# A two-trunk encoder layer on one core: stores of neighbourhood attention by SyncE, strips dealt per unit, a weight load behind rope rows, two token sums in another tile

## The chip, the cores and the metric

One Trainium2 chip, and one of its cores. The metric is the device time of one execution in microseconds, the median of the runs shown. Lower is better. A core has five engines that work beside each other, each in the order of its own queue: TensorE (PE in the profile), VectorE (DVE), ScalarE (ACT), GpSimd (POOL) and SyncE (SP, which issues transfers and computes nothing). ACT and POOL can issue transfers too.

## The reference

One encoder layer, run on two inputs with shared weights: `x_prompt` (1024 tokens, the "long" trunk) and `x_sample` (512 tokens, the "short" trunk), both 1024 wide, float32. Cut to what matters:

```python
def _token_mixer(xn, ...):
    z = xn @ w_in                     # q_A k_A v_A q_B k_B v_B gate_A gate_B
    qa = rope(rmsnorm(qa)); ka = rope(rmsnorm(ka))
    o_a = _gqa_attention(qa, ka, va)              # all tokens, 8 heads
    o_b = _neighbourhood_attention(qb, kb, vb, rpb)   # 8 heads, a window of the token grid
    merged = sigmoid(ga) * (o_a @ w_proj_a) + sigmoid(gb) * (o_b @ w_proj_b)
    return merged @ w_out

def _trunk(x, ...):
    h = x + _token_mixer(_rmsnorm(x, norm_mix_g), ...)
    h = h + (relu(_rmsnorm(h, norm_mlp_g) @ w_mlp_up) ** 2) @ w_mlp_down
    return _rmsnorm(h, norm_final_g)
```

The neighbourhood attention takes 128 queries at a time against a band of rows of the 64-wide token grid, adds a learned bias per head and 2-D offset, masks what is outside the window, and takes the softmax.

## The kernel before

**Arithmetic.** Every float32 product is made of three PE products of a high and a low part (`mm3`, whose one line is L216, so nearly all of PE's rows carry that line). High parts come from ACT (L203 for weights, L1594 in the MLP), low parts from DVE (L210, L1595).

**Stages.** `run` works the short trunk (number 0 in the program's names, NT=4 token tiles, NB=1), then the long one (number 1, NT=8, NB=2). Each has four: R (norm, rotary rows, projections, in two groups g), A (global attention), B (neighbourhood attention, 32 units of head h and query block j in the order 1, 2, 0, 3), G (gated merge, `w_out`, the sum with x, the norm for the MLP). One MLP over all tokens follows.

**What orders the work.** Within the code's dependences a scheduler of the framework sets the order on each engine at build, by its own estimate of costs. `tc.keep_in_program_order` and `tc.issue_after` pin an instruction. On the chip each engine then runs its fixed list. Transfers issued by SP and ACT share eight completion semaphores, dealt in turn at build: an issue also waits until the transfer that had its semaphore before has landed, and whatever stands behind it on its engine waits too.

**Short B.** For a head, `prep` fetches its bias rows (`rects`, L1080) and 16 value strips (`vss`, L1094, from the DRAM scratch `vds`). A unit then is: scores (`sbs`, PE), bias, mask and maximum (DVE L1193), exponential (ACT L1222, out `pbs`), scaling of the rows (POOL L1225), transposition (PE L1266, back into `sbs`), high and low parts (ACT L1273, DVE L1274), and values times weights (`obs<-bhs,vss`, PE). `finish_o` copies the outcome (ACT L482, `ot_Bs`) and stores it to the scratch `obds`. Between units PE takes pieces of gate products (`gpss`, out `sgs`, ACT L470), which are stored to the scratch `zgs`. Both stores go through `put` (L441), here from ACT's queue. POOL builds the next head's masked bias (`bms`, L1173) and copies key rows by a transfer (L1157).

**Long R, g=0.** For token tile tt: the tile `xts` (L280) is squared and normed (ACT L300, DVE L304), transposed (PE L317, `ptxs`), split (ACT L327, DVE L333), multiplied (`zs`); then rotary rows `rts` (L745, three buffers) enter on POOL L705 and DVE L716, and ACT L721 makes `rrs`, which PE transposes (L642, `pqs`). The first gate weights of g=0 (`raw_gs`, 512 KB, L249) are asked for by `fill.pull(1)` in the code of tile 6; the scheduler had put the load ahead of the fifth tile's.

**Long G, second half, token tiles 4 to 7.** The tile `xrs` (x's columns, L1487) gets the `w_out` product added (DVE L1527) and is stored by POOL (L1528, `hd<-xrs`). It lies in the ring `k4` of four tiles. The norm's weights `gb` (`gbms`) are last read at tile 3 of this half. In the MLP's start, `S` and `A` tiles lie on memory that G has left: the fifth and seventh `A` of the first products on that of tiles 6 and 7.

Of the kernel before, what the change touches and what calls it, by code (L numbers as in the profile page):

```python
# [61 lines left out]
def encoder(ctx: ExitStack, tc: tile.TileContext, xs, outs, w):  # L62
# [362 lines left out]
    def run(tr, nxt, first):  # L425
        N, x, T, NT, NB = tr.N, tr.x, tr.T, tr.NT, tr.NB
# [8 lines left out]
        fill = Fill()  # L435
        later_put, slot_no = [], [None]
# [109 lines left out]
        for g in range(2):  # L546
            with phase(f"phR{N}_{g}") as ph:
                xn_of, pre = {}, {}
                fresh = g == 0 and tr.ready < NT
                if fresh and not first:  # L550
# [13 lines left out]
                    gb = ph.tile([P, 1, D], F32, tag="gb", name=f"gb{N}", bufs=1)  # L564
                    row_bcast(gb, w["norm_mix_g"], D)
                    gb = gb[:, 0]
# [3 lines left out]
                elif fresh:  # L570
                    gb = ph.tile([P, D], F32, tag="gb", name=f"gb{N}", bufs=1)
# [149 lines left out]
                        nc.scalar.activation(rr[:, i, :], t[:, h, :], AF.Copy, scale=r[:, h : h + 1])  # L721
                    rr_of[tt] = rr

                lag, x_rest = [], []
                for tt in range(NT):
                    tb, j = divmod(tt, 4)
                    nm = f"{N}_{g}_{tt}"
                    def next_tile():
                        rest = tr.p0_t(tt + 1, xn_of.pop(tt + 1))
                        if not first:  # L730
                            x_rest[:] = [rest]
                        if not first and tt + 3 < NT:
                            next_norm(tt + 3)
                        elif first and tt + 2 < NT:
                            step = held.pop(0) if held else None
                            xn_of[tt + 2] = tr.p0(tt + 2, ph, gb, xt_of.get(tt + 2), step)
                            while held:
                                held.pop(0)()

                    to_come = fresh and tr.ready <= tt + 1 < NT  # L740
                    in_z = first and to_come and tt > 0
                    if to_come and not in_z:
                        next_tile()
                    rt = pre.pop("rt", None) or ph.tile([P, 2, HD], F32, tag="rt", name=f"rt{nm}", bufs=3)
                    op = nc.sync.dma_start(rt, w["rope"][tt * P : (tt + 1) * P])  # L745
                    if first and fresh and tt < 2:
                        tc.keep_in_program_order(op)
                    z = mm(f"z{nm}")[:, :384]
                    js = slice(j * P, (j + 1) * P)

                    for c0, c1 in ((0, 256), (256, 384)) if first and g + tt == 0 else ((0, 384),):
                        for k in range(NC8):
                            mm3(
                                z[:, c0:c1],
                                xh(tb, k)[:, js],
                                xl(tb, k)[:, js],
                                wh[k // 4][:, k % 4, c0:c1],
                                wl[k // 4][:, k % 4, c0:c1],
                                k == 0,
                                k == NC8 - 1,  # L760
                            )
                            if in_z and k == 2:
                                next_tile()
                    if tt >= 2:
                        values(tt - 2)
                        heads_t(tt - 2)
                    lag.append(partial(chain, tt, z, rt))
                    if not (first and fresh) or tt > 0:
                        lag.pop(0)()
                    if tt == NT - 1:  # L770
                        while lag:
                            lag.pop(0)()
                    if fresh and not first:
                        if tt == 0:
                            xn_of[tr.ready] = norm_to(xn_next, xt, gb, f"{N}_{tr.ready}")
                            tr.p0_t(*tr.carry.pop(0))
                        if tt == 1:
                            next_norm(tr.ready + 1)
                    if first and g == 0 and tt == 1:
                        load_pad()  # L780
                    if tt == NT - 2:
                        fill.add(gate(2304, zg[0], g * 4, g * 4 + 4))
                        fill.pull(1)

                if g == 0:
                    warm_table(AF.Exp, rr_of[NT - 1][:, 0, 0:1], f"e{N}")
# [11 lines left out]
            with phase(f"phA{N}_{g}") as ph:  # L798
# [148 lines left out]
                else:  # L947
# [4 lines left out]
                    for ui, u in enumerate(units):  # L952
                        h, qb = u
# [106 lines left out]
        with phase(f"phB{N}") as ph:  # L1060
# [4 lines left out]
            n = len(units)  # L1065
            moved = set(units[: n - 8]) if NB == 2 else set()
# [6 lines left out]
            def prep(h):  # L1073
                prep_bias(h)
                for j in range(4):
                    prep_v(h, j)

            def prep_bias(h):
                rc = ph.tile([P, 16, 48], F32, tag="rect", name=f"rect{N}_{h}", bufs=2)
                nc.sync.dma_start(rc, biases[:, :, h].rearrange("r c i j -> (r c) i j"))  # L1080
                rects[h] = rc
# [249 lines left out]
                due_t.setdefault(i + ls, []).append(u)  # L1331
                due_v.setdefault(i + ls + 1, []).append(u)
            for i in range(n + 4 - NB):
                if moved:
                    slot_no[0] = i
                if i < n - 8:
                    f = (5 if i < 2 else 2 + i % 2) if NB == 1 else 5 - (i % 6 == 5)
                else:
                    f = 3 if NB == 1 else 8
                if NB == 2 and i == n - 11:  # L1340
                    pa = proj_a(ph, raw_here)
                    next(pa)
                spare.clear()
                if i < n:
                    late = i > 0 and units[i - 1] in moved
                    if i > 1 and units[i - 2] in moved:
                        fetch_t(units[i - 2])
                    s_unit(units[i], partial(turn, units[i - 1]) if late else None)
                    h, j = units[i]
                    if j == 1 and h < 7:  # L1350
                        if moved:
                            prep_bias(h + 1)
                        else:
                            prep(h + 1)
                    if moved and h > 0:
                        with behind("SP"):
                            prep_v(h, j)
                    if i % 8 == 6 and i + 2 < n:

                        qp = qkproj(i // 8 + 1, wqk, qk)  # L1360
                        for _ in range(NC8):
                            next(qp)
                    if i % 8 == 7 and qp is not None:
                        for _ in qp:
                            pass
                        qp = None
                        if i + 1 < n - 8:
                            wqk = load_qk(i // 8 + 2, held)
                if NB == 2 and i == n - 7:
                    for u in due_v.pop(i):  # L1370
                        v_unit(u)
                    fill.drain()
                    fill.add(pa)
                fill.pull(f // 2)
                for u in due_t.get(i, ()):
                    t_unit(u)
                if NB == 1 and i == n - (12 if first else 8):
                    pa = proj_a(ph, raw_here)
                    next(pa)
                if NB == 1 and i == n - 8:  # L1380
                    fill.drain()
                    fill.add(pa)
                if held and (i in (4, 5) if i < 8 else i % 8 in (2, 4)):
                    held.pop(0)()
                if i == 3:
                    wqk = load_qk(1, held)
                if oa_held and i >= (n - 9 if NB == 2 else n - 11):
                    oa_held.pop(0)()
                if qp is not None and NB == 2:
                    for _ in range(NC8):  # L1390
                        next(qp)
                fill.pull(f - f // 2)
                for u in due_v.get(i, ()):
                    v_unit(u)
                if NB == 2 and oa_held and i >= n - 9:
                    oa_held.pop(0)()
                while later_put and later_put[0][0] < i:
                    nc.sync.dma_start(*later_put.pop(0)[1:])
# [8 lines left out]
        with phase(f"phG{N}") as ph:  # L1407
# [55 lines left out]
            gb = ph.tile([P, 1, D], F32, tag="gb", name=f"gbm{N}", bufs=1)  # L1463
            row_bcast(gb, w["norm_mlp_g"], D)
            gb = gb[:, 0]
# [7 lines left out]
            for half in range(2):  # L1473
                wo = wos[half]
                hc = slice(half * 512, half * 512 + 512)
                for tt in range(NT):
                    tb, j = divmod(tt, 4)
# [2 lines left out]
                    rows_ = slice(r0, r0 + P)  # L1480

                    later = half == 1 and nxt is None and tb == 1
                    if later:
                        xr = ph.tile([P, D], F32, tag="k4", name=f"xr{nm}", bufs=4)[:, 0:512]
                    else:
                        xr = tmp_zs(f"xr{nm}")
# [44 lines left out]
                    if half == 1:  # L1531
# [12 lines left out]
                        else:  # L1544
# [10 lines left out]
                            if 3 <= tt <= 5:  # L1555
                                j = tt - 3
# [563 lines left out]
```

## Time and profile before

| | |
|---|---|
| median of 3 runs | 2090.06 us (2089.89 to 2092.77) |
| the profiled execution | 2093.47 us |
| its span, first to last instruction | 2091.7 us |
| mean granted PE clock | 0.998 |
| busy: PE, DVE, ACT, POOL | 2067.3, 1457.4, 1140.2, 447.4 us |

All times in the profile are of the one profiled execution, in us from its span's start. A timeline row reads: start, duration, engine, line, operation, `out<-in`, shapes, how many in a row; the bracket at its end is the engine's idle time just before and what ended it. A queue's name ends in q (SPq, ACTq) where the row is the issue of a transfer. Names are the program's, with their numbers left out.

### The profile page before, as it was taken

What the parts mean: (1) busy time and instruction counts of PE and PEld (TensorE: products, weight loads), DVE (VectorE), ACT (ScalarE), POOL (GpSimd) and SP (SyncE); (2) the same over time, 40 slices, a digit from 0 to 9 for tenths busy, and PEclk for the clock granted to TensorE, in tenths of its full rate; (3) what the DMA queues carried; (4) which work ended last, traced back from release to release, by engine and by line L of the source; (5) the groups of instructions that cost most, each with busy time, mean ns of one, the idle gap of its engine ahead of it and who ended that gap; (6) DMA issues with size and microseconds to landing.
All of it is one profiled execution on the core that took longest, in us unless ns stands there. A gap on an engine that the chain in (4) does not pass through costs nothing.

```text
span 2091.7 us, 31228 instructions
## 1 busy us (share of the span) xinstructions
PE 2067.3 (99%) x10615; PEld 1813.4 (87%) x10615; DVE 1457.4 (70%) x2691; ACT 1140.2 (55%) x2455; POOL 447.4 (21%) x556
## 2 busy tenths in 40 slices
PE   9999999999999999999999999999999999999998
PEld 8887778887898788888888999999999988888887
DVE  6665786778448646778845777787777777669663
ACT  6674663668557735556413565565656634334442
POOL 2323310317724753443002000011000000000000
PEclk9999999999999999999999999999999999999999
DMA  6537557548628867767544556487545899678561
GB/s 194 148 112 198 168 161 254 190 136 223 169 66 217 215 182 212 219 224 215 186 167 166 183 176 211 152 246 208 159 151 161 291 334 348 216 263 277 170 211 61
DMA packets 407910, 409.99 MB, mean 196 GB/s; under 512 B 98367, under 2 KB 334919, under 8 KB 407751
## 3 DMA queue, kind: packets, MB, share of 16 engines
q1 hardware_dynamic: 368119, 339.16, 52.6%
q10 hardware_dynamic: 29408, 41.96, 5.9%
q0 software_dynamic: 10224, 26.88, 4.9%
q8 instruction: 84, 1.38, 0.3%
q14 instruction: 75, 0.61, 0.1%
HBM read 294.21 MB, written 114.49 MB: 195 GB/s over the span
## 4 chain that ended last, share of the span: by engine, by line
PE 77%; DVE 1%; issue 1%; DMA 1%; ACT 1%; POOL 0%; SPq 0%; POOLq 0%; DVEq 0%; ACTq 0%
PE dn L216 20%; PE gpss L216 8%; PE ud L216 6%; PE ua L216 6%; PE uc L216 6%; PE ops L216 3%; PE ub L216 3%; PE zs L216 2%; PE ppbs L216 2%; PE pqbs L216 2%; PE pkbs L216 2%; PE ppas L216 2%; PE zvs L216 2%; PE dnf L216 2%; PE ss L810 1%; PE ss L811 1%
## 5 line engine op out<-in xcount | busy, mean ns | idle before, releaser
L216 PE MATMUL dn<-wd,ah 128*128 128x512 f32 x1248 | 384.1, 389 | 0.0
L216 PEld LDWEIGHTS dn<-wd,ah 128*128 128x128 f32 x1248 | 234.3, 188 | 48.4
L216 PE MATMUL dn<-wd,al 128*128 128x512 f32 x624 | 242.8, 389 | 0.0
L1594 ACT ACTIVATE ah<-ar 128x512 fp32r<-128x512 f32 x168 | 103.8, 627 | 193.9 <-PE dn L216 174.4
L216 PE MATMUL gpss<-xs_0h,w_gs 128*128 128x512 f32 x512 | 185.5, 399 | 0.0
L1595 DVE TENSOR_TENSOR al<-ar,ah 128x512 fp32r<-128x512 f32 x168 | 113.9, 686 | 71.7 <-ACT ah L1594 63.8
L216 PE MATMUL ud<-B,A 128*128 128x384 f32 x768 | 145.0, 337 | 2.3 <-DVE c L1712 2.3
L216 PE MATMUL uc<-B,A 128*128 128x384 f32 x768 | 143.7, 334 | 0.0
L216 PE MATMUL ua<-B,A 128*128 128x384 f32 x768 | 139.0, 334 | 0.0
L216 PEld LDWEIGHTS dn<-wd,al 128*128 128x128 f32 x624 | 117.2, 188 | 24.4
L216 PEld LDWEIGHTS ud<-B,A 128*128 128x128 f32 x768 | 135.1, 189 | 2.6 <-DVE c L1712 2.6
L216 PEld LDWEIGHTS uc<-B,A 128*128 128x128 f32 x768 | 134.0, 188 | 0.2 <-ACT A L1594 0.2
L216 PEld LDWEIGHTS ua<-B,A 128*128 128x128 f32 x768 | 134.0, 188 | 0.2
L180 POOL TENSOR_TENSOR rs_f<-ms_f,mhalf 128x1 f32<-128x1 f32 x6 | 4.0, 666 | 590.7 <-DVE ms_f L176 590.7
L813 DVE TENSOR_REDUCE nms<-ss 128x1 f32<-128x1024 f32 (+1 forms) x96 | 99.3, 1037 | 32.5 <-PE ss L811 32.2
L216 PE MATMUL ops<-wh_os,mgs 128*128 128x512 f32 x384 | 119.5, 391 | 0.0
L822 ACT ACTIVATE ps<-ss,nms 128x1024 f32<-128x1024 f32 (+1 forms) x96 | 93.3, 973 | 38.5 <-DVE nms L813 37.4
L216 PEld LDWEIGHTS gpss<-xs_0h,w_gs 128*128 128x128 f32 x512 | 96.0, 188 | 17.4
L216 PE MATMUL gpss<-xs_0l,w_gs 128*128 128x512 f32 x256 | 101.0, 394 | 0.0
L1594 ACT ACTIVATE A<-S 128x512 fp32r<-128x512 f32 x128 | 75.9, 623 | 32.1 <-DVE S L1657 23.3
L216 PE MATMUL gpss<-xs_1h,w_gs 128*128 128x512 f32 x256 | 90.8, 393 | 0.0
L1225 POOL TENSOR_SCALAR pbs<-pbs,rlbs 128x384 f32<-128x384 f32 (+1 forms) x96 | 72.1, 756 | 85.1 <-DVE rlbs L1224 75.4
(309 smaller groups left out, 5161.0 us busy)
## 6 DMA issues: line engine op xcount, KB each, us to landing
ar<-ud SPq DMA_DIRECT2D x120, 512.0 KB, 5.5
br<-in_w_mlp_down_dram SPq DMA_DIRECT2D x72, 512.0 KB, 5.4
rawu<-in_w_mlp_up_dram SPq DMA_DIRECT2D x64, 512.0 KB, 4.1
ud<-c ACTq DMA_DIRECT2D x128, 192.0 KB, 3.4
raw_gs<-in_w_in_dram SPq DMA_DIRECT2D x32, 512.0 KB, 3.9
tas<-ps SPq DMA_DIRECT2D x32, 512.0 KB, 3.3
hqs<-tas SPq DMA_DIRECT2D x32, 512.0 KB, 5.5
ud<-cs SPq DMA_DIRECT2D x64, 192.0 KB
```

Of the source, the lines that this page charges most:

```text
L180: op = nc.gpsimd.tensor_tensor(r[:, :n], m[:, :n], mhalf[:, :n], op=ALU.pow)
L216: op = nc.tensor.matmul(out, a, b, **kw)
L810: nc.tensor.matmul(s[:, ks], lhs, kT[:, 0, ks], start=True, stop=False)
L811: nc.tensor.matmul(s[:, ks], lhs, kT[:, 1, ks], start=False, stop=True)
L813: nc.vector.tensor_reduce(nm_, s, axis=AX.X, op=ALU.max, negate=True)
L822: op = nc.scalar.activation(to, of, AF.Exp, bias=nm_, accum_out=l)
L1225: nc.gpsimd.tensor_scalar(p, p, rl, 1.0, op0=ALU.mult, op1=ALU.mult)
L1594: nc.scalar.activation(hi, src, AF.Copy)
L1595: nc.vector.tensor_tensor(lo, src, hi.bitcast(F32), op=ALU.subtract)
```

## The change

Three places, in four edits.

1. Short B, stores: for the first 16 of the 32 units `put` no longer issues from ACT but leaves the store in `later_put`, which the loop empties into SP's queue one unit later. The last 16 units store from ACT as before.
2. Short B, strips: the next head's bias rows are still asked for at its predecessor's first unit, but its 16 strips are dealt four to a unit (`prep_v(h + 1, j)`).
3. Long R, g=0: the first gate-weight load is held back with `tc.issue_after` until the issue of the fourth tile's rotary rows.
4. Long G, second half: token tiles 6 and 7 put their sums into the two halves of `gb`'s tile in place of two tiles of the ring.

```diff
-                lag, x_rest = [], []
+                lag, x_rest, ropes = [], [], []
...
                     op = nc.sync.dma_start(rt, w["rope"][tt * P : (tt + 1) * P])
+                    ropes.append(op.ins)
...
                         fill.add(gate(2304, zg[0], g * 4, g * 4 + 4))
-                        fill.pull(1)
+                        with tc.issue_after(ropes[3]) if fresh and not first else nullcontext():
+                            fill.pull(1)
...
             for i in range(n + 4 - NB):
-                if moved:
-                    slot_no[0] = i
+                slot_no[0] = i if moved or i < n // 2 else None
...
                     if j == 1 and h < 7:
-                        if moved:
-                            prep_bias(h + 1)
-                        else:
-                            prep(h + 1)
+                        prep_bias(h + 1)
+                    if not moved and h < 7:
+                        prep_v(h + 1, j)
...
                     later = half == 1 and nxt is None and tb == 1
-                    if later:
+                    if later and tt >= NT - 2:
+                        xr = gb[:, (tt - NT + 2) * 512 : (tt - NT + 3) * 512]
+                    elif later:
                         xr = ph.tile([P, D], F32, tag="k4", name=f"xr{nm}", bufs=4)[:, 0:512]
```

`moved` is empty in the short trunk and holds units in the long one, so edits 1 and 2 leave the long B as it was. Lines behind L724 shift by up to two in the changed kernel (L1222 is L1224 there, L441's stores on SP carry L1398).

**ACT in short B, about the first gate store.** In a row before (the numbers behind `pbs` are trunk, head, query block):

```order
L203 ACTIVATE w_gs0_3328_2_2291<-raw_gs0_3328_2_0_2289 128x1024
L470 ACTIVATE sgs0_3328_0_0_2286<-gpss0_3328_0_0_2246 128x512
L441 DMA zgs0_1_100<-sgs0_3328_0_0_2286 128x512
L1222 ACTIVATE pbs0_0_0_2307,lbs0_0_0_0_2308<-sbss0_0_0_0_2304,nmbs0_0_0_0_2305 128x256
L1273 ACTIVATE bhs0_0_1_2316<-sbs0_0_0_2299 128x2x128
```

and now:

```order
L203 ACTIVATE w_gs0_3328_2_2282<-raw_gs0_3328_2_0_2280 128x1024
L470 ACTIVATE sgs0_3328_0_0_2278<-gpss0_3328_0_0_2234 128x512
L1224 ACTIVATE pbs0_0_0_2298,lbs0_0_0_0_2299<-sbss0_0_0_0_2295,nmbs0_0_0_0_2296 128x256
L1275 ACTIVATE bhs0_0_1_2311<-sbs0_0_0_2290 128x2x128
L1224 ACTIVATE pbs0_0_3_2331,lbs0_0_3_0_2332<-sbss0_0_3_0_2328,nmbs0_0_3_0_2329 128x256
```

The store is gone from between the gate's sigmoid piece and the third unit's exponential; in the same way every store of the first 16 units is gone from ACT's list.

**SP in short B, the strips of heads 1 and 2.** Before:

```order
L249 DMA raw_bqs0_2_0_2588<-in_w_in_dram 128x8x128
L1094 DMA vss0_1_2226<-vds0_98 32x2x128 x16
L1094 DMA vss0_2_2385<-vds0_98 32x2x128 x16
L249 DMA raw_bks0_2_0_2591<-in_w_in_dram 128x8x128
L249 DMA raw_gs0_3328_4_0_2608<-in_w_in_dram 128x8x128
L1080 DMA rects0_3_2637<-biases_97 128x768
L249 DMA raw_gs0_3328_5_0_2765<-in_w_in_dram 128x8x128
```

and now, from the last strips of head 2 on:

```order
L1096 DMA vss0_2_2384<-vds0_98 32x2x128 x4
L1398 DMA obds0_102<-ot_Bs0_0_0_2456 64x128
L1096 DMA vss0_2_2384<-vds0_98 32x2x128 x3
L249 DMA raw_bks0_2_0_2590<-in_w_in_dram 128x8x128
L249 DMA raw_gs0_3328_4_0_2606<-in_w_in_dram 128x8x128
L1082 DMA rects0_3_2635<-biases_97 128x768
L1398 DMA obds0_102<-ot_Bs0_0_3_2522 64x128
L249 DMA raw_gs0_3328_5_0_2763<-in_w_in_dram 128x8x128
```

Between the load that heads the first piece and the strips that head the second stand nine rows now: 25 strips, and among them two gate stores and two stores of `ot_Bs`. Loads that had nothing computed ahead of them (`raw_bks`, `raw_gs`, `rects0_3`) now stand behind stores of head 0's units.

**SP in long R.** Before (`xts1_4` is the fifth token tile, `rts1_0` the rotary rows of the first):

```order
L1494 DMA xas0_1_3_4482<-in_x_prompt_dram 128x1024
L249 DMA raw_gs1_2304_0_0_5276<-in_w_in_dram 128x8x128
L109 DMA gbs1_4556<-in_norm_mix_g_dram 128x1024
L280 DMA xts1_4_4558<-in_x_prompt_dram 128x1024
L745 DMA rts1_0_4552<-in_rope_dram 128x128
L745 DMA rts1_0_1_4669<-in_rope_dram 128x128
L280 DMA xts1_5_4724<-in_x_prompt_dram 128x1024
L745 DMA rts1_0_2_4733<-in_rope_dram 128x128
L745 DMA rts1_0_3_4851<-in_rope_dram 128x128
L249 DMA raw_gs1_2304_1_0_5448<-in_w_in_dram 128x8x128
```

and now:

```order
L1496 DMA xas0_1_3_4482<-in_x_prompt_dram 128x1024
L109 DMA gbs1_4556<-in_norm_mix_g_dram 128x1024
L280 DMA xts1_4_4558<-in_x_prompt_dram 128x1024
L745 DMA rts1_0_4552<-in_rope_dram 128x128
L745 DMA rts1_0_1_4669<-in_rope_dram 128x128
L280 DMA xts1_5_4724<-in_x_prompt_dram 128x1024
L745 DMA rts1_0_2_4733<-in_rope_dram 128x128
L745 DMA rts1_0_3_4851<-in_rope_dram 128x128
L249 DMA raw_gs1_2304_0_0_5276<-in_w_in_dram 128x8x128
L280 DMA xts1_6_4842<-in_x_prompt_dram 128x1024
```

The gate weights moved from ahead of the norm weights and the fifth tile to behind the fourth tile's rotary rows; the second gate load moved behind `xts1_6`, the third behind `rts1_0_4`. In the long G only names change on SP, DVE and POOL (`gbms1` where `xrs1_1_6` and `xrs1_1_7` stood).

## The prediction

> **What bounds the kernel now.** The page's busy times and its chain come first.
>
> ```profile
> span 2091.7 us, 31228 instructions
> ...
> PE 2067.3 (99%) x10615; PEld 1813.4 (87%) x10615; DVE 1457.4 (70%) x2691; ACT 1140.2 (55%) x2455; POOL 447.4 (21%) x556
> ...
> PE 77%; DVE 1%; issue 1%; DMA 1%; ACT 1%; POOL 0%; SPq 0%; POOLq 0%; DVEq 0%; ACTq 0%
> ```
>
> PE is busy for all but 2091.7 − 2067.3 = 24.4 us, and the chain of the last end runs through it. The change removes no PE work, so it can win only PE's idle time at its three places, and PE time at a low clock. So I read PE's timeline there for brackets, and went from each back to what came last. 0.2% (4.2 us) is about what a measurement of this kernel can tell from no change.
>
> **Short B.** PE's gaps there:
>
> ```profile
> 188.66 0.41 PE L1266 MATMUL sbs<-ident,pbs 128*128 128x128 f32 x2 [1.42 <-DVE nmbs L1193]
> ...
> 219.85 0.41 PE L1266 MATMUL sbs<-ident,pbs 128*128 128x128 f32 x2 [1.74 <-DVE nmbs L1193]
> ...
> 222.79 0.41 PE L1266 MATMUL sbs<-ident,pbs 128*128 128x128 f32 x2 [0.24 <-POOL pbs L1225]
> ```
>
> The named releaser is the mean's DVE step, but between it and PE stands ACT's exponential, and ACT's timeline shows why that was late:
>
> ```profile
> 182.92 0.60 ACT L470 ACTIVATE sgs<-gpss 128x512 f32<-128x512 f32 x1
> 186.34 0.33 ACTq L441 DMA_DIRECT2D zgs<-sgs  x1
> 186.84 0.51 ACT L1222 ACTIVATE pbs<-sbss,nmbs 128x256 f32<-128x256 f32 x1 [3.32 <-DMA kBs<-kBs]
> ...
> 216.88 0.45 ACTq L441 DMA_DIRECT2D obds<-ot_Bs  x1
> 217.43 0.38 ACT L482 ACTIVATE ot_Bs<-obs 64x256 f32<-64x256 f32 x1 [2.93 <-DMA vss<-vds]
> 217.71 0.50 ACT L1222 ACTIVATE pbs<-sbss,nmbs 128x256 f32<-128x256 f32 x1
> ```
>
> The gate piece was done at 183.52, but its store was issued at 186.34, and ACT computed nothing for 3.32 us. The second time it was 2.93 us, put down to a strip's transfer: the store's completion semaphore still belonged to it. The exponential stood behind the store both times. Without the store the first exponential can start near 183.5, the second about 2.9 us earlier, both more than PE's gap. So edit 1 takes away 1.42 + 1.74 = 3.16 us. I count 3.1; the 0.24 behind POOL stays out of the sum and in the range.
>
> What it costs stands on SP.
>
> ```profile
> L1094 SPq DMA_DIRECT2D vss<-vds x112: 302/426/1267, 179.7 to 282.7; - x112
> L216 PE MATMUL obs<-bhs,vss x64: 274/281/386, 190.3 to 304.3; 128*128 128x256 f32 x64
> ...
> DMA to landing us min/median/max: 1.7/1.9/3.5
> ...
> 199.41 0.88 SPq L1080 DMA_DIRECT2D rects<-biases  x1
> ...
> 206.43 0.67 POOL L1173 TENSOR_TENSOR bms<-rects,msks 128x256 f32<-128x256 f32 x1 [7.34 <-DMA rects<-biases]
> ...
> 213.72 0.57 POOL L1157 DMA_DIRECT2D kBs<-kBs  x1 [6.16 <-DVE rlbs L1224]
> ```
>
> The 64 value products take 114.0 us, two for a unit, so a unit takes 114.0/32 = 3.6 us and a head 14.3. Strips of a later head are now asked for a head ahead, in fours: four issues at the median 0.43 and a landing of 1.9 are 3.6 us, against 14.3 of lead. Edit 2 by itself I cost at nothing; that lead is its cover, and if SP fell 10.7 us behind, PE would wait for strips, 1 us for 1 us. SP does fall behind compute: its list now waits for each of the stores. `rects0_3`, for which POOL already waited 7.34 us, now stands behind the store of head 0's third unit. That unit's value product comes near 190.3 + 2 × 3.6 = 197.5, its copy a microsecond or so later, then three strips and two loads: near 201 by my estimate, 2 us later than 199.41. On POOL the row scaling of head 1's last unit no longer stands behind that `bms`, and after it POOL idles 6.16 us until the key copy at 213.72: this covers 2 us. The bound is 0 if all is covered, and 1 us for 1 us past 6.16. The eighteen stores that leave ACT took 0.33 to 0.45 us of issue each; on SP they add about 7 us over 60, and only their waits matter. Stores of the last 16 units stay on ACT, and hold semaphores that SP's strips had, now issued closer to them: the nearest rows are the two stalls above, so a new one costs up to 1.74, or nothing if PE has gate or query work beside it. I take 0, and keep −3.6 to +2 for the whole place.
>
> **Long R.**
>
> ```profile
> raw_gs<-in_w_in_dram SPq DMA_DIRECT2D x32, 512.0 KB, 3.9
> ...
> 376.80 0.37 SPq L249 DMA_DIRECT2D raw_gs<-in_w_in_dram  x1
> 377.22 1.04 SPq L109 DMA_DIRECT2D gbs<-in_norm_mix_g_dram  x1
> 378.30 1.05 SPq L280 DMA_DIRECT2D xts<-in_x_prompt_dram  x1
> 379.51 1.76 SPq L745 DMA_DIRECT2D rts<-in_rope_dram  x2
> ...
> 385.56 1.09 ACT L327 ACTIVATE xs_0h<-ptxs 128x512 fp32r<-128x512 f32 x2 [1.15 <-PE ptxs L317]
> 389.01 1.06 ACT L300 ACTIVATE xns<-xts 128x1024 f32<-128x1024 f32 x1 [2.36 <-DMA xts<-in_x_prompt_dram]
> ...
> 389.94 1.16 POOL L705 TENSOR_TENSOR us<-ts,rts 128x160 f32<-128x160 f32 x2 [6.94 <-DMA rts<-in_rope_dram]
> ...
> 386.64 0.48 DVE L696 TENSOR_TENSOR ts<-zs,gtab 128x320 f32<-128x320 f32 x1
> ...
> 393.15 0.33 PE L642 MATMUL pqs<-ident,rrs 128*128 128x128 f32 x1 [0.76 <-ACT rrs L721]
> 394.21 0.52 PE L317 MATMUL ptxs<-ident,xns 128*128 128x128 f32 x3 [0.25 <-DVE ms_As L176]
> ...
> 403.25 0.44 PE L216 MATMUL zs<-wghs,xs_1l 128*128 128x384 f32 x1 [1.35 <-DVE xs_1l L333]
> ```
>
> The gate load went out at 376.80, ahead of norm weights, fifth tile and rotary rows. ACT was done at 386.65 and waited until 389.01 for the tile; POOL waited for rotary rows until 389.94, while its other input was ready at 387.12. PE's three gaps after that, 0.76 + 0.25 + 1.35 = 2.36 us, are this lateness travelling down the two chains. Without 512 KB ahead, and with norm weights and tile asked for earlier by SP's wait before 376.80, both inputs need to come only 2.4 and 2.8 us earlier. The fewest they move is the queue's time for one such transfer: the page has 3.9 us for a median gate load from issue to landing, so I take the full 2.36, of which I count 2.4. Bounds: 0 if rotary rows are held by something else, 2.8 if PE gains all of POOL's 389.94 − 387.12. The moved load itself is next late: it goes out behind the fourth tile's rotary rows, whose buffer is the first tile's, free when POOL's first L705 is done. That ends at 391.10 before, so near 388.5 now, and the load and the two behind it go out in the next microseconds. Its first use:
>
> ```profile
> 423.35 1.08 ACT L203 ACTIVATE w_gs<-raw_gs 128x1024 fp32r<-128x1024 f32 x1
> ```
>
> That is some 35 us later, so it costs nothing; past that it would cost 1 for 1. The sixth and seventh tiles have one gate load ahead of them, as before.
>
> **G's tail and the MLP's start.**
>
> ```profile
> 1150.40 0.69 DVE L1527 TENSOR_TENSOR xrs<-ops,xrs 128x512 f32<-128x512 f32 x1 [2.31 <-PE ops L216]
> ...
> 1151.86 0.55 POOL L1528 DMA_DIRECT2D hd<-xrs  x1
> ...
> 1152.51 2.19 ACT L1594 ACTIVATE A<-S 128x512 fp32r<-128x512 f32 x4 [6.95 <-PE ua L216]
> 1156.83 1.68 ACT L1594 ACTIVATE A<-rawu 128x512 fp32r<-128x512 f32 x3 [2.12 <-DMA hd<-xrs]
> 1158.78 0.48 ACT L1725 ACTIVATE s<-uc 128x384 f32<-128x384 f32 x1
> ...
> 1157.49 1.90 DVE L1595 TENSOR_TENSOR A<-rawu,A 128x512 fp32r<-128x512 f32 x3 [1.46 <-ACT A L1594]
> ...
> 1164.65 3.77 PE L216 MATMUL ud<-B,A 128*128 128x384 f32 x12 [2.27 <-DVE c L1712]
> ...
> 215.00:220.00 5.00, 3.27 (x19) 2.46 (x18) 2.98 (x8) 2.52 (x7) 1.59 (x3) 1.00 0.62 135
> ...
> 1165.00:1170.00 5.00, 5.00 (x22) 5.00 (x21) 3.67 (x7) 3.06 (x7) 0.00 (x0) 0.66 0.35 125
> ```
>
> The store of tile 7's sum, issued at 1151.86, held the memory that the fifth and seventh `A` need, so ACT waited 2.12 us and DVE behind it 1.46. DVE has almost no idle from there to `c`, which frees PE after 2.27 us. Edit 4 frees that memory: DVE moves 1.46 earlier, PE's gap falls to 0.81. Then the clock (the last window's eighth column): 0.66 over 5 us is 5 × 0.34 = 1.7 us of lost PE work, directly behind the gap; the window with the 1.74 us gap shows 1.00. A gap of 0.81 should not lower it, so 1.46 + 1.70 = 3.16, counted 3.2. The stores' new place, `gb`, is written next by the `s` of `uc`, in before at 1158.78, 1.9 us after the stores let go (ACT's start at 1156.83); ACT now comes there with 0 to 2 us less to spare but waits for the same PE product, so I cost it at nothing. Ends: 0 if it waits as long as `A` did, 4.0 if the whole gap goes.
>
> [...]
>
> **Sum.** 3.1 + 2.4 + 3.2 = 8.7 us off the profiled execution's 2093.47 gives 2084.8. That execution is 3.4 above the median, so on the median of 2090.06 it is 2081.4 (0.42% faster).
>
> **Rivals.** *Stores make SP the late queue* (slower). Place: `rects0_3` and `rects0_4`, behind stores. From the point where they come more than 6.16 us later, POOL's key copy and the next head's products slip 1 for 1. To end above +4.2 the loss must pass 8.7 + 4.2 = 12.9 us, say 12.6 us later for each of the two: about 2100. For it: POOL's wait of 7.34. Against: the estimate of 2. Chance 0.06.
>
> *Stalls move to the second half of short B.* A store of a late unit waits on ACT for a strip, as at 216.88: one or two of them give back what edit 1 won, and the time is 2081.4 + 3.1 = 2084.5. For it: those stores still issue from ACT. Against: strips land 1.9 us after issue, and SP issues fewer in a row. 0.17.
>
> *The clock drop stays*, since 0.81 us of idle suffices or the drop has another cause: 2081.4 + 1.7 = 2083.1. Against it: the 1.74 us gap at full clock. 0.12.
>
> *Rotary rows are not sooner*: SP waits for another buffer: 2081.4 + 2.4 = 2083.8. For it: the issue at 379.51 includes a wait. 0.08.
>
> *Two of these at once, or a cost I have not seen*: 8.7 shrinks to under 4.2; 2087. The median of before spans 2089.89 to 2092.77. 0.15.
>
> **Chances and range.** The forecast keeps 0.42. Faster by over 0.2% are the forecast and the three single rivals: 0.42 + 0.17 + 0.12 + 0.08 = 0.79, less 0.04 for errors of size in these: 0.75. Within 0.2%: 0.15 + 0.04 = 0.19. Slower: 0.06. The forecast alone ranges over 2079 to 2083 (all small gaps of the two first places and the whole 2.27 give 2081.4 − 0.5 − 0.4 − 0.8 = 2079.7, and the median's lower end is 0.2 lower). The range reaches to 2087.5, which takes in single rivals and half of the mixed case, and to 2078.
>
> **What would show it.** Right: no ACT gap of 3 us behind L470 near 184 or before L482 near 215; POOL L705 near 387; PE's `ud` near 1163 with a bracket under 1 and a window at 1.00. Wrong: an ACT bracket over 1.5 near 255 to 285 put down to `vss`; POOL L1175 waiting over 10 us; ACT L1725 waiting for `hd<-gbms`; PE's busy time longer than before.

## The result, and the profile after

The changed kernel took 2086.59 us in the median of 21 runs (2085.33 to 2089.66), the kernel before 2091.28 in as many (2087.00 to 2094.54). The ratio is 0.9982, its 95% interval 0.9975 to 0.9989: faster by 0.18%, about 3.8 us (2.3 to 5.2) of 2091, or 4.7 by the medians. The forecast was 8.7. The three places changed as described, and the two profiles at hand, 2091.7 and 2084.8 us of span, lie 6.9 apart. So the question is not whether the waits went but how large they usually are.

The page of the changed kernel:

```profile
span 2084.8 us, 31252 instructions
...
PE 2065.9 (99%) x10615; PEld 1811.7 (87%) x10615; DVE 1457.2 (70%) x2691; ACT 1141.5 (55%) x2455; POOL 449.9 (22%) x556
```

PE's idle time is 2084.8 − 2065.9 = 18.9 us against 24.4, and its busy time is 1.4 us less, at the same work. Nearly all of that is in the `ud` products (145.0 us on the page before, 143.7 now), some of which ran at half clock before (granted clock 0.50 for 3.4 us from 1165.20 on).

Short B, ACT's timeline at the two places that stalled:

```profile
183.05 0.60 ACT L470 ACTIVATE sgs<-gpss 128x512 f32<-128x512 f32 x1
185.22 0.51 ACT L1224 ACTIVATE pbs<-sbss,nmbs 128x256 f32<-128x256 f32 x1 [1.57 <-DVE nmbs L1195]
...
213.57 1.05 ACT L203 ACTIVATE w_bqs<-raw_bqs 128x1024 fp32r<-128x1024 f32 x1
214.55 0.51 ACT L1224 ACTIVATE pbs<-sbss,nmbs 128x256 f32<-128x256 f32 x1
```

No store stands between, ACT waits only for its input, and PE has no bracket over 0.2 us from 170 to 300. Long R, timelines of SP, ACT and POOL:

```profile
370.14 0.42 SPq L109 DMA_DIRECT2D gbs<-in_norm_mix_g_dram  x1
373.11 0.33 SPq L280 DMA_DIRECT2D xts<-in_x_prompt_dram  x1
376.75 0.84 SPq L745 DMA_DIRECT2D rts<-in_rope_dram  x2
...
386.73 0.38 SPq L249 DMA_DIRECT2D raw_gs<-in_w_in_dram  x1
...
383.89 1.06 ACT L300 ACTIVATE xns<-xts 128x1024 f32<-128x1024 f32 x1
...
384.56 1.18 POOL L705 TENSOR_TENSOR us<-ts,rts 128x160 f32<-128x160 f32 x2 [4.21 <-DVE ts L696]
```

The fifth tile is there when ACT comes, and POOL waits for DVE and no longer for rotary rows. The gate load goes out at 386.73. The MLP's start, timelines of ACT and PE and two windows:

```profile
1150.76 1.66 ACT L1596 ACTIVATE A<-rawu 128x512 fp32r<-128x512 f32 x3
...
1159.25 2.37 PE L216 MATMUL ud<-B,A 128*128 128x384 f32 x12 [0.72 <-DVE c L1714]
...
1155.00:1160.00 5.00, 4.28 (x25) 3.96 (x24) 5.00 (x10) 2.44 (x5) 0.00 (x0) 1.00 0.62 202
1160.00:1165.00 5.00, 5.00 (x31) 5.00 (x30) 3.18 (x6) 3.96 (x10) 0.00 (x0) 1.00 0.35 124
```

ACT does not wait for the stores, PE's gap is 0.72 and the clock stays at 1.00. New in this profile are two waits of PE far from the change, in long A and long B (rows of the waits):

```profile
PE os L846 <- ACT pths L862: 1.1, 1, 1.1
PE obs L216 <- DVE mAs L1052: 1.0, 1, 1.0
```

Behind both stands a load that landed late: ACT waited 1.31 us for `hqs<-tas` and 3.67 us for `raw_pas`. Theory 1: such waits, and those of short B and long R before, change from one execution to the next, and the prediction was sized on a bad one. Theory 2: the change causes the two new ones, and they give back what it won.

### The profile page after: what moved, and what is told of

Read it like the earlier page. It is cut to its first block, busy times and chain, and to the rows that moved or that the text cites. A ratio compares the mean times of both kernels' runs of the same rounds, so it can differ in the third digit from the quotient of the medians.

```text
span 2084.8 us, 31252 instructions
## 1 busy us (share of the span) xinstructions
PE 2065.9 (99%) x10615; PEld 1811.7 (87%) x10615; DVE 1457.2 (70%) x2691; ACT 1141.5 (55%) x2455; POOL 449.9 (22%) x556
## 5 line engine op out<-in xcount | busy, mean ns | idle before, releaser
L216 PE MATMUL ud<-B,A 128*128 128x384 f32 x768 | 143.7, 334 | 0.7 <-DVE c L1714 0.7
L216 PE MATMUL uc<-B,A 128*128 128x384 f32 x768 | 143.7, 334 | 0.0
```

What stands on the lines that cost most here:

```text
L216: op = nc.tensor.matmul(out, a, b, **kw)
```

## The experiments

Every ratio below is to the kernel before, run on the same chip. Each run also left a profile, and the sums of PE's gaps in them are set side by side further down.

**The kernel before, again.** No edit.

> The kernel before, unchanged, as a control. Theory 1 (the 8.7 us were summed on one execution that was itself slower than its kind by a low-clock stretch and by chance waits of a transfer): the gaps of 1.42, 1.74, 0.76 + 0.25 + 1.35 and about 2.3 us recur at their places within 0.3 us, the 3.4 us at half clock behind the last one is there in some executions and not in others, and waits that the changed kernel's profile showed in long A (near 521) and long B (near 960), 1.1 and 1.0 us, can show here too. Theory 2 (the change causes those two waits): here the first is at most 0.3 us and the second is absent, as in the first profile of before. Time: ratio 1.000 within 0.001 by both.

Measured: ratio 1.0004 (0.9995 to 1.0013). PE in short B, ACT there, then ACT and PE in long R:

```profile
188.91 0.41 PE L1266 MATMUL sbs<-ident,pbs 128*128 128x128 f32 x2 [0.54 <-DVE nmbs L1193]
218.82 0.41 PE L1266 MATMUL sbs<-ident,pbs 128*128 128x128 f32 x2 [0.46 <-DVE nmbs L1193]
222.49 0.41 PE L1266 MATMUL sbs<-ident,pbs 128*128 128x128 f32 x2 [0.95 <-DVE nmbs L1193]
...
187.10 0.51 ACT L1222 ACTIVATE pbs<-sbss,nmbs 128x256 f32<-128x256 f32 x1 [2.45 <-DMA kBs<-kBs]
216.41 0.38 ACT L482 ACTIVATE ot_Bs<-obs 64x256 f32<-64x256 f32 x1 [1.64 <-PE sbs L1266]
...
386.53 1.06 ACT L300 ACTIVATE xns<-xts 128x1024 f32<-128x1024 f32 x1 [0.22 <-DMA xts<-in_x_prompt_dram]
...
400.53 0.44 PE L216 MATMUL zs<-wghs,xs_1l 128*128 128x384 f32 x1 [0.39 <-DVE xs_1l L333]
...
1163.13 3.91 PE L216 MATMUL ud<-B,A 128*128 128x384 f32 x12 [2.68 <-DVE c L1712]
```

The same instructions wait, but for 0.54 + 0.46 + 0.95 where the first profile had 1.42 + 1.74 + 0.24, and ACT's wait for the fifth tile is 0.22 and not 2.36. My expectation that those gaps would recur within 0.3 us failed. The ud gap, 2.68 after 2.27, came back at its place and size, give or take 0.4. So the sizes of the first two terms change with when transfers land: the gate load that the fifth tile followed took, by the transfers' rows of the first and of the third profile of before,

```profile
raw_gs<-in_w_in_dram SPq DMA_DIRECT2D x1, 512.0 KB, 8.9
```

```profile
raw_gs<-in_w_in_dram SPq DMA_DIRECT2D x1, 512.0 KB, 6.9
```

us from issue to landing. Those 2 us agree with ACT's wait for the tile behind it, 2.36 us in the one and 0.38 in the other. POOL's wait for rotary rows stayed in the third profile, and PE's largest gap in long R was still 1.24 us there:

```profile
388.68 1.17 POOL L705 TENSOR_TENSOR us<-ts,rts 128x160 f32<-128x160 f32 x2 [5.38 <-DMA rts<-in_rope_dram]
```

**Each place alone.** The diff's parts one by one: edits 1 and 2; edit 3; edit 4.

> Edits 1 and 2 alone. Theory 1: PE's gaps of short B (0.16 + 1.42 + 1.74 + 0.24) go to under 0.4 us in all, nothing else moves, time 3.1 us less (ratio 0.9985). Theory 2: as much is won there, but the wait of PE for ACT L860 in long A near 523 grows to about 1 us and the one in long B near 963 appears, so the time falls by 1.3 us (0.9994).

> Edit 3 alone. Theory 1: the three gaps of long R (2.36 us) go, no gap over 0.3 us behind 390, time 2.4 us less (ratio 0.9989). Theory 2, if this edit is the cause (it moves the gate weights of long A): PE's gap in long A near 524 is about 1 us, and the time falls by 1.4 us (0.9993).

> Edit 4 alone. Theory 1: PE's gap before the MLP's ud falls from 2.27 to 0.7 us and no half-clock stretch follows it. Time: 1.5 us less if the typical execution of before has no half-clock stretch there, 3.2 if it has one always (ratios 0.9993 and 0.9985). [...]

Measured: 0.9992 (0.9983 to 1.0001), 0.9987 (0.9978 to 0.9996), 0.9985 (0.9976 to 0.9994). Each removes its own gaps and leaves those of the other two places; the waits of about 1 us near 521 and 960 came with none of them (none and 0.13 us with edits 1 and 2, 0.22 and 0.26 with edit 3, 0.38 and none with edit 4), against theory 2. The intervals are too wide to size a single part: together the three say 7.5 us, with some 1.9 either way on each.

**The changed kernel again, and without edit 4.**

> The changed kernel, unchanged, as a control. Theory 1 (waits for a transfer's landing change from one execution to the next, and the profile of before was a bad one): the two waits of the changed kernel's first profile, 1.1 us in long A near 521 and 0.96 us in long B near 960, do not both recur; PE's gaps outside start, short B, long R and the ud gap, 5.2 us there, come to 3 to 5 us. Short B under 0.5 us, long R under 0.5, ud 0.7, no half-clock stretch. Theory 2 (the change causes those two): both recur within 0.3 us. Time: 0.25% under before (5.2 us) by theory 1's typical gains of 1.5 + 0.5 + 3.3 us.

> Edits 1 to 3 without edit 4. By theory 1 the two places together give 1.5 to 2.5 us (ratio 0.9990), not the 5.5 of the prediction (0.9974): PE's gaps in short B and long R are under 0.5 us each, the ud gap stays at 2.3 to 2.7 us and the half-clock stretch of 3.4 us behind it is there. By the prediction's own sizes the ratio is 0.9974.

Measured: 0.9980 (0.9972 to 0.9989) and 0.9994 (0.9985 to 1.0003). The two waits did not recur in size: 0.46 us at 522 and 0.12 at 964. But the gaps outside the three places and the start came to 6.1 us, more than the 3 to 5 that I had expected. Without edit 4 the first three edits give 1.3 us, and their forecast 5.5 (0.9974) lies outside the interval. Short B of the changed kernel is not clean, though. ACT and PE in this second profile:

```profile
248.93 0.52 ACTq L441 DMA_DIRECT2D obds<-ot_Bs  x1
249.50 0.51 ACT L1224 ACTIVATE pbs<-sbss,nmbs 128x256 f32<-128x256 f32 x1 [1.24 <-DVE w_bqs L210]
...
251.90 0.50 PE L216 MATMUL obs<-bhs,vss 128*128 128x256 f32 x2 [0.71 <-DVE bhs L1276]
```

This is the first store that remains on ACT, that of head 3's second unit (a unit's outcome comes up to three turns of the loop later, so 16 turns take 13 of these stores off ACT), and it stalls ACT as the earlier ones did: the row names DVE, but ACT was done at 248.26, and the semaphore of the store in front came free only at 248.86, when a strip (`vss`) landed.

**Which edit of short B.** Edit 2 alone, then edit 1 alone.

> Edit 2 alone, on the kernel before: strips dealt in fours, stores on ACT. Theory 1: the stores stay where they were, so PE's gaps of short B are those of before, 1.3 to 3.7 us, and the ratio is 1.000. Rival (the bursts of strips on SP were what held ACT's stores): the gaps fall under 0.6 us and the ratio is 0.9993. Long R and the MLP's start are those of before here: 0.5 to 2.6 us of gaps and a ud gap of 2.3 to 2.7 with a half-clock stretch of 3.4 us.

> Edit 1 alone, on the kernel before: stores of 16 units on SP, strips asked for 16 at a time. Theory 1: PE's gaps near 187 and 218 go (under 0.3 us), what remains in short B is 0.1 to 1 us near 250; ratio 0.9993. Rival (stores on SP are safe only with dealt strips): strips or bias rows come late behind stores, and PE's gaps in short B are over 1 us, with POOL's wait for rects over 9 us. Long R and the MLP's start as in before.

Measured: 0.9996 (0.9987 to 1.0005) and 0.9990 (0.9981 to 0.9999). With dealt strips alone PE's gaps are 0.94 and 2.24 us, as before; with the stores alone there is 0.12 near 185, none near 218, and 1.13 near 250, behind the same store that stays on ACT. The stores are the edit that acts.

**More stores on SP.** One condition replaced in the changed kernel, in each of three runs by one of the lines with a plus (the remarks behind them are mine):

```diff
-                slot_no[0] = i if moved or i < n // 2 else None
+                slot_no[0] = i                                            # all 32 units
+                slot_no[0] = i if moved or i < n // 2 + 3 else None       # 19 units
+                slot_no[0] = i if moved or i < 3 * n // 4 else None       # 24 units
```

> The changed kernel with all 32 units' stores on SP. In three of six profiles with edits 1 and 2, PE waited 0.14 to 0.93 us near 250 for DVE's low parts, where ACT stood in front of the first store that stays with it until a gate-merge load on the same completion semaphore had landed (247.85 and 248.66 in the two worst, 246.3 to 247.1 where PE did not wait). Theory 1 (any store on ACT is held by whatever transfer had its semaphore before): without stores on ACT this wait is gone, PE's gaps in short B come to 0.1 to 0.3 us, and the kernel is 0.3 us faster than the changed one on average (ratio to before 0.9979). Rival (SP becomes the late queue): SP's bias rows and projection weights now wait for 16 more units' outcomes, and PE waits over 0.5 us for POOL or for ppas between 255 and 306.

> The changed kernel with the stores of 19 units on SP in place of 16. If the wait left in short B near 250 is the store in front of which ACT stands, it goes (PE's gaps in short B 0.1 to 0.3 us in all), the end of short B near 306 stays at 0.2, and the kernel is 0.3 to 0.5 us faster than the changed one. If SP is late already, POOL or ppas waits for it instead and nothing is gained.

> The same with 24 units. If the loss of all 32 units lay only in the rows of the last units' outcomes, read back at the end of short B (1.3 us near 306, with a half-clock stretch), then with 24 that end is at 0.2 and the gaps of short B are 0.1 to 0.3: as fast as with 19. If it grows with each store that SP takes over, PE waits 0.3 to 1 us between 255 and 306, and it is slower than with 19.

Measured: 0.9993 (0.9984 to 1.0002) with 32, 0.9979 (0.9970 to 0.9989) with 19, 1.0001 (0.9992 to 1.0010) with 24. With 19 the wait near 250 shrank to 0.13, but my expectation of 0.1 to 0.3 us for all of short B failed: its gaps came to 3.11. PE, ACT and SP there:

```profile
254.05 0.41 PE L1268 MATMUL sbs<-ident,pbs 128*128 128x128 f32 x2 [1.42 <-DVE nmbs L1195]
...
290.74 0.41 PE L1268 MATMUL sbs<-ident,pbs 128*128 128x128 f32 x2 [1.07 <-DVE nmbs L1195]
...
252.73 0.38 ACT L482 ACTIVATE ot_Bs<-obs 64x256 f32<-64x256 f32 x1 [2.72 <-DMA obds<-ot_Bs]
...
242.72 7.35 SPq L1096 DMA_DIRECT2D vss<-vds  x6
250.49 0.45 SPq L1398 DMA_DIRECT2D obds<-ot_Bs  x1
```

This is another stall than before. ACT issues no store there. It waits to overwrite one of the three `ot_Bs` tiles, and the store out of that tile is now SP's: SP took 7.35 us over six strips ahead of it, issued it at 250.49, and ACT went on at 252.73 when it had landed. So here SP is the late queue of the rival, by way of the tile that a late store holds. What ended the second gap, near 290, was not followed. With 32, the lateness shows at the end of short B, where the last heads' rows are read back: ACT waited 0.75 us for those rows (`rawos<-obds`) and 0.79 for weights (`raw_pbs`), not told apart here, and PE waited 1.30 and ran at half clock after that (PE, then a window, whose eighth column is the clock):

```profile
307.45 4.84 PE L216 MATMUL ppbs<-oXs,w_pbs 128*128 128x512 f32 x13 [1.30 <-DVE oXs L210]
...
305.00:310.00 5.00, 3.66 (x10) 2.40 (x11) 3.45 (x10) 2.17 (x4) 0.00 (x0) 0.79 0.71 226
```

With 24 about the same wait, 1.31 us, stands near 308, without a half-clock stretch in that profile. ACT waited 2.7 us in three pieces for `ot_Bs` tiles as with 19, and PE 0.96 near 260. Of the two outcomes that I had named, the second came: PE waits between 255 and 306 too, and 24 is slower than 19. It does not simply grow with the stores, since 32 is not slower than 24. No number of stores beats 16 clearly. (The first of these three expectations names a gate-merge load as what held the store near 250. By the semaphores of the trace it was the strip named above.)

**The sums, halved.** Only tile 7 in the norm weights' tile, on the kernel before.

```diff
+                    if later and tt == NT - 1:
+                        xr = gb[:, 0:512]
-                    if later:
+                    elif later:
```

> Edit 4 halved, on the kernel before: only token tile 7's sum lies in the norm weights' tile, tile 6's stays in the ring. Theory 1: what the A tiles waited for was the store of tile 7 alone (issued at 1151.86; tile 6's, at 1150.76, had let go before ACT came), so ACT does not wait over 0.5 us, PE's gap before ud is 0.7 us and no half-clock stretch follows: ratio 0.9985 as with edit 4. Rival (tile 6's store lands late enough too): ACT waits 1 us or more and the gap is 1.2 to 2 us. Short B and long R are those of before.

Measured: 0.9986 (0.9977 to 0.9995). ACT and PE:

```profile
1152.38 1.66 ACT L1596 ACTIVATE A<-rawu 128x512 fp32r<-128x512 f32 x3
...
1160.87 2.37 PE L216 MATMUL ud<-B,A 128*128 128x384 f32 x12 [0.72 <-DVE c L1714]
```

ACT follows its own work without a bracket: tile 7's store alone was the wait.

**A longer gap.** In the changed kernel, two or four steps that change no value are added on DVE, ahead of `put(1, 1, d, s5)`, to make PE wait longer (the remark is mine):

```diff
+            for _ in range(4 if st == (0, 0) else 0):      # 2 in the other run
+                nc.vector.tensor_tensor(s5, s5, s5, op=ALU.max)
```

> The changed kernel with two maxima of the tile s with itself ahead of c in the MLP's first step, which leave every value as it is and add about 0.5 us each on DVE: PE's gap before ud is about 1.7 us. [...]

> The same with four: PE's gap before ud is about 2.7 us, as in before, with the changed kernel's memory. If the gap itself is the cause of the half-clock stretch, 3.4 us at half clock follow it and the span is longer than the changed kernel's by 2.0 + 1.7 us; if the cause was something else at this place (the transfers, the memory), no half-clock stretch follows. [...]

Measured: 0.9981 (0.9971 to 0.9991) and 0.9983 (0.9973 to 0.9993). The gap before ud was 0.79 and 0.90 us in place of the 1.7 and 2.7 expected, since the scheduler put 7 and 13 products of the next step ahead of it, so these two say nothing on the clock.

**Third profiles.**

> The kernel before, a third profile. By the theory that the first profile of before was a bad one at two of the three places: PE's gaps in short B near 185 to 223 come to 1.3 to 2.5 us (3.6 in the first), those of long R behind 390 to 0.5 to 1.4 (2.6 in the first), the ud gap to 2.3 to 2.7. By the prediction's sizes: 3.2 or more and 2.4 or more.

> The changed kernel, a third profile: short B 0.1 to 1.0 us, by where the load on the first remaining store's semaphore lands; long R 0.3; ud 0.7, no half-clock stretch near 1160; the gaps outside these places and the start 3.5 to 6 us, at places that differ from the first two profiles.

Measured: 2093.86 and 2087.42 us in one run each. Both profiles came as expected by theory 1, but for long R of before with 1.52 us where at most 1.4 was expected. The sums of PE's gaps of 0.1 us or more by place, in us (short B from 170 to 300, long R from 390 to 415, ud in the MLP's first step, and what follows that gap), for the kernels in which a place is as in before (a place that is changed is left empty or has a dash):

| profile | short B | long R | ud gap | half clock behind ud |
|---|---|---|---|---|
| first of before (the prediction's) | 3.66 | 2.64 | 2.27 | 3.4 us |
| before again; third | 2.13; 2.48 | 0.68; 1.52 | 2.68; 2.43 | 3.4; 3.4 |
| edits 1+2 alone | | 0.60 | 2.38 | 3.4 |
| edit 3 alone | 1.32 | | 2.50 | 3.4 |
| edit 4 alone; one sum moved | 1.58; 2.24 | 1.35; 0.94 | | |
| strips alone; stores alone | 3.30; – | 1.20; 1.20 | 2.30; 2.32 | none; 3.4 |
| edits 1 to 3 | | | 2.46 | 3.4 |

With the edits: short B 0.12, 0.90 and 0.20 in three profiles of the changed kernel, and 0.37, 0.28, 1.22, 0.19 in the others with edits 1 and 2 at 16 units; long R 0.27 to 0.41 in ten; ud 0.72 to 0.75 in eight (0.79 and 0.90 in the two with added work), and no half clock behind it.

## Why the prediction was right or wrong

**Short B: the mechanism right, the size wrong.** Counted at 3.1 us. The five profiles with neither edit, without the first, have 1.95 us on average; with both edits the seven have 0.47. The term is 1.5 (1.7 if the run with dealt strips alone, whose stores stood as before, is counted in). The step that failed is the one that took 1.42 + 1.74 from one execution as the gap's size. A quarter of a microsecond on average is also the rival *Stalls move to the second half*, given a chance of 0.17: it happens in some executions, at 250, for 0 to 0.9 us. The covers held in the changed kernel: POOL's wait for bias rows cost PE nothing, and dealing the strips was worth nothing by itself. *SP the late queue* did not come true at 16 units. SP was late with 19, 24 and 32, and at other places than I named: not bias rows, but the tiles that late stores hold and, it seems, the rows read back at the end. (The time that I gave for that rival, about 2100, did not follow from its terms: 2081.4 + 12.9 is 2094.)

**Long R: the mechanism right, the size wrong.** Counted at 2.4. The step that failed is the same: PE's 2.36 us of one execution were taken as the usual size. The seven profiles with that place as in before, without the first, have 1.07; with edit 3 the ten have 0.30. The term is 0.8. In four of the seven POOL still waited for rotary rows, and PE's gaps were 0.94 to 1.52; in two it waited for DVE instead, and they were 0.60 and 0.68. The bound that I used for the least shift, 3.9 us for a gate load, was no help, since it says how far the inputs move and not how late they usually are. The moved load cost nothing, as argued.

**G's tail: right.** Counted at 3.2. The gap fell from 2.44 (mean of seven without the first) to 0.73, 1.7 us, and 1.7 us of half clock went in seven profiles of eight, 1.5 on average: 3.2. That the total is the one forecast is in part luck, since its parts were put at 1.46 and 1.70. Edit 4 alone measured 3.1 (1.3 to 5.0), and half of it 2.9. The store's new place made no one wait. The rival *The clock drop stays* is refuted at this place.

**Sum.** 1.5 + 0.8 + 3.2 = 5.5, against 2.3 to 5.2 and 2.3 to 5.9 measured in the two comparisons of the changed kernel: a little above the first, inside the second. That the first profile was 2.2 us over the median that 21 runs gave was visible only afterwards; the prediction saw it 3.4 above a median of three and still took every gap of it in full. Its two variable places held 1.7 and 1.6 us more than usual, and that is most of what was missing.

**A part of theory 2 stays.** One small wait outside the three places does recur: near 718 in long A, PE waited 0.21 to 0.84 us (0.60 on average) in all seven profiles with edits 1 and 2 at 16 units, and 0.11 or less in the eleven others, among them the three with 19, 24 and 32 units. ACT in the second profile of the changed kernel, and in the first of before:

```profile
717.08 1.06 ACT L908 ACTIVATE hqs<-hqs 128x1024 fp32r<-128x1024 f32 x1 [2.60 <-DMA hqs<-tas]
```

```profile
718.59 1.06 ACT L906 ACTIVATE hqs<-hqs 128x1024 fp32r<-128x1024 f32 x1 [0.68 <-DMA hqs<-tas]
```

The transfer lands later there, though SP's list is the same at that place. Why was not tried and stays open; with it the sum is 4.9, inside both intervals. Open too is why the same 512 KB load takes 6.5 to 6.9 us in seven executions and 8.9 in an eighth, the first.

## What to carry to other kernels

Of three gaps that all go back to a transfer's landing, one recurred (2.3 to 2.7 us in eight profiles) and two were draws from a spread (1.3 to 3.7 and 0.6 to 2.6). The kind of the wait did not tell them apart. Behind the one that recurred is a store that landed 4.9 to 5.4 us after its issue in all eight, so ACT's wait for it, 2.12 us in the first profile, was much the same in the next:

```profile
1155.31 1.67 ACT L1594 ACTIVATE A<-rawu 128x512 fp32r<-128x512 f32 x3 [2.53 <-DMA hd<-xrs]
```

So before pricing an edit, read the gap in two or three profiles, also those of other variants that leave the place alone, and price it by their mean. A store on a computing engine's queue stalled that engine when the transfer that it waited behind was late: by the semaphores of the first profile of before, the store at 186.34 followed a strip on the same semaphore that landed at 186.26, and the one at 216.88 a gate-merge load (the prediction has a strip there) that landed at 216.80, and ACT stood idle for 3.32 and 2.93 us. Moving some of the stores can pass the stall to the next that remains (0 to 1.1 us of PE's time near 250 here). Moving more of them had its own price: a store that was late on SP held the tile it reads, and ACT waited 2.72 us to write that tile (19 units).

## What the runs showed of the hardware

The half-clock stretch (granted clock 0.5 in the trace's records) was 3.4 us long wherever it came ahead of the last microseconds of the span, but the gap's length alone did not tell whether it came. It followed a gap of 1.30 us (with 0.12 before it) in the kernel with all stores on SP, as shown. With the strips alone it followed the gap in short B and did not follow the longer one before ud (PE and a window each, from that profile):

```profile
219.80 0.66 PE L1266 MATMUL sbs<-ident,pbs 128*128 128x128 f32 x2 [2.24 <-DVE nmbs L1193]
...
220.00:225.00 5.00, 5.00 (x23) 4.32 (x23) 3.71 (x12) 2.85 (x10) 2.66 (x4) 0.71 0.46 136
...
1166.42 2.37 PE L216 MATMUL ud<-B,A 128*128 128x384 f32 x12 [2.30 <-DVE c L1711]
...
1165.00:1170.00 5.00, 3.58 (x20) 3.59 (x21) 4.15 (x8) 3.44 (x7) 0.00 (x0) 1.00 0.44 140
```

In the first profile of before, the window from 220 to 225, behind the gap of 1.74 us, is at 1.00 too. So the stretch followed gaps of 1.30 us, of 2.24, and of 2.27 to 2.68 before ud in seven profiles; it did not follow 1.31 (24 units), 1.74 and 2.30. What decides besides the length, no run shows.
